# Scores of a query block as three products and then three copies, heads 0 to 3 ranked in twos, and five gathers issued inside the query phase

## The chip, the cores and the metric

The kernel runs on one core of one Trainium2 chip. The metric is device time in microseconds (us) of one execution, and the time of a version is the median of several runs. The engines are named as in the profile: PE is TensorE (matrix products), DVE is VectorE, ACT is ScalarE, POOL is GpSimd, SP is SyncE, which only issues transfers. Each engine runs its own instructions in the order in which the program lists them; semaphores make one engine wait for another.

## The reference

One layer of a hybrid decoder for 336 tokens, all in fp32. A mixer (a Conformer convolution and a Mamba-2 SSD side by side) is followed by PEER, a mixer of experts that are looked up with product keys. The change touches PEER alone:

```python
def peer_block(xb, w_q, keys, U, V):
    T = xb.shape[0]
    q = (xb @ w_q).reshape(T, PEER_HEADS, 2, D_KEY // 2)
    s = jnp.einsum('thcd,hckd->thck', q, keys).astype(jnp.float32)
    s1, i1 = lax.top_k(s[:, :, 0], PEER_TOPK)
    s2, i2 = lax.top_k(s[:, :, 1], PEER_TOPK)
    cand = (s1[..., :, None] + s2[..., None, :]).reshape(T, PEER_HEADS, PEER_TOPK * PEER_TOPK)
    sc, f = lax.top_k(cand, PEER_TOPK)
    ids = (jnp.take_along_axis(i1, f // PEER_TOPK, axis=-1) * N_KEYS
           + jnp.take_along_axis(i2, f % PEER_TOPK, axis=-1))
    g = jax.nn.softmax(sc, axis=-1)
    act = jax.nn.gelu(jnp.einsum('thkd,td->thk', U[ids], xb).astype(jnp.float32), approximate=False)
    w = (g * act).astype(xb.dtype)
    return jnp.einsum('thk,thkd->td', w, V[ids])
```

There are 8 heads with two halves each, 128 keys in each half, 16,384 experts, and 16 experts for each head and token, so 128 picks for each token. A row of U and a row of V have 1024 numbers.

## The kernel before

The mixer takes the first 527 us and isn't touched. PEER needs 320 of the tokens, and the kernel serves them in two ways. 128 *gathered* tokens (and 8 more, packed sixteen picks to a column) get their experts' rows by indirect transfers: for one pick of each of the 128 tokens a gather (L1159) brings 128 rows of U and V side by side, 1 MB, into one of five buffers `wuv`; VectorE makes the dot with the token (`pick_dot`, L1317), ScalarE takes the Gelu of it (L1319) and multiplies it by the softmax weight (L1322), and VectorE adds the weighted V rows to `ygat` (`pick_sum`, L1327). That is 137 steps. The other 184 *dense* tokens go through all experts: TensorE multiplies 128 blocks of U (512 KB each, L1429), ScalarE takes the Gelu into `S` (L1431), a mask with the weights is multiplied in, and TensorE multiplies 128 blocks of V (L1531).

**Query phase** (the loop over `j` of 16 blocks, 8 heads by 2 halves). A block of `w_q` (512 KB, from the SP queue) is split into a high half `wh`, made by ScalarE (L249), and a low half `wl`, made by POOL in four pieces of 128x256 (L253). TensorE makes 16 products of 128x320 with `wh` and 8 with `wl` (L182) into a PSUM tile `pj`; ScalarE copies that to `qT` (L1202). Then TensorE multiplies it by the keys, once for each of three tiles of tokens: the gathered 128, 128 dense ones, and 64 more (tile `psc`, L1206). ScalarE copies each of the three to SBUF (L1208): to `sco` for the gathered tokens, to `sall` for the others. All three products share one PSUM tile, and the program writes product, copy, product, copy; a product that writes `psc` waits for the copy of the product before it.

**Ranking.** `top16` (five steps of VectorE, L1061 to L1069) ranks the gathered tokens' scores as each block comes. After block 7, `heads_tasks(0)` works on heads 0 to 3: the sums of the two halves (`cand`), their top 16, the ids and the softmax weights (`gid` at L1136, `ggw`). Then `ahead(0)` issues the first gathers on POOL. The gathered tokens' heads 4 to 7 and the dense tokens' rankings (`topk_tasks(1)`, `topk_tasks(2)`) follow in the U phase.

**U phase.** Between the U blocks a `Feed` hands out VectorE's tasks (rankings and pick steps) by their cost, so many for each block: `NU = (42, 26, 35)` says how many picks fall to the first 84 U blocks, the other 44, and the first part of the V phase; the remaining 34 come last. A gather's buffer is free when the sum of the pick five before it has run. U outputs go to six PSUM banks in turn. U blocks land in eight tiles `pre` and a ring of eight `eraw` slots; from block 25 on every odd block is issued on ScalarE's queue (L1412). A dependency written by hand keeps every ranking of dense tokens behind the first cast to `gid` (`early[0]`), and one keeps each pick's Gelu behind the last score copy (`scored`).

A scheduler with a simulated timeline sets the order of instructions on each engine out of this program; it is the order below.

## Time and profile before

| | |
|---|---|
| median of 3 runs | 1280.56 us (1278.71, 1280.62, 1280.56) |
| the profiled execution | 1278.62 us, its span 1276.8 us |
| granted TensorE clock, mean | 0.995 of full speed |
| query phase | from about 529 us; U phase to 929 us, V phase behind it |
| TensorE busy | 1257.3 us of the span |
| VectorE, ScalarE, GpSimd busy | 961.7, 520.4, 595.6 us |

The profile is of one execution. Its rows give start and duration in us, the engine, the line of the kernel, the operation, what it writes and reads, and how many instructions a row holds; in brackets is how long the engine stood idle before and what ended that. A matmul of fp32 has two records for one product; TensorE is pipelined, so the distance of two starts, not the duration, is what a product costs.

### The profile page before, as it was taken

Reading aid. Unit: us, or ns where it says so; the run is one execution under the profiler, and the core shown is the slowest. Engines: PE = TensorE matmul, PEld = TensorE weight load, DVE = VectorE, ACT = ScalarE, POOL = GpSimd, SP = SyncE. Lnnn points to the kernel's source line nnn. Section 1 sums busy time; section 2 is a strip of 40 time slices with the busy share of each in tenths; the row PEclk is TensorE's granted clock in tenths of the full one; section 3 lists DMA queues with packets and bytes.
Section 4 is the critical chain, followed back from the end, with each engine's and each line's share of the span. In section 5 each row is a group of like instructions: output and inputs, shape, how many; then the busy total and the mean of one; then the engine's idle time right before and its main releaser. Section 6 shows DMA issues by size and latency. Waiting matters only on the chain.

```text
span 1276.8 us, 23637 instructions
## 1 busy us (share of the span) xinstructions
PE 1257.3 (98%) x8953; PEld 1214.0 (95%) x8953; DVE 961.7 (75%) x2121; ACT 520.4 (41%) x1308; POOL 595.6 (47%) x595
## 2 busy tenths in 40 slices
PE   9999999999999999999999999999999999999997
PEld 7989999999889999999999999999999999999997
DVE  6888889888977335549999978888888888545555
ACT  6778777887766444544232222222210111001102
POOL 2487777887795766975132232223322322122110
PEclk9899999999999999999999999999999999999999
DMA  6435454344434444765989999999999999999994
GB/s 248 166 130 194 158 190 169 140 175 170 145 126 149 149 150 149 255 243 210 372 321 422 421 420 420 420 420 420 420 421 420 420 421 419 397 421 420 419 421 158
DMA packets 85618, 373.82 MB, mean 293 GB/s; under 512 B 9585, under 2 KB 15089, under 8 KB 65921
## 3 DMA queue, kind: packets, MB, share of 16 engines
q1 hardware_dynamic: 48048, 166.87, 34.9%
q0 software_dynamic: 19584, 142.62, 26.9%
q10 hardware_dynamic: 17872, 62.84, 12.2%
q8 instruction: 70, 1.15, 0.4%
q14 instruction: 44, 0.35, 0.1%
HBM read 359.24 MB, written 13.05 MB: 292 GB/s over the span
## 4 chain that ended last, share of the span: by engine, by line
PE 81%; DVE 15%; DMA 2%; ACT 1%; issue 1%; POOL 1%; ACTq 0%; DVEq 0%
PE pj L182 32%; PE va L1531 25%; PE pj L1429 15%; DVE wuv L1317 2%; DVE ygat L1327 2%; PE pg L1457 2%; DVE pcv L525 1%; PE pst L182 1%; DMA wuv<-in_peer_uv_dram,gid 1%; PE po L182 1%; PE py L182 1%; PE pq L182 1%; DMA wdt<-in_w_dt_dram 1%; DVE st L718 1%; DVE si L1066 1%
## 5 line engine op out<-in xcount | busy, mean ns | idle before, releaser
L1159 POOL DMA_INDIRECT wuv<-in_peer_uv_dram,gid x136 | 166.2, 1222 | 478.3 <-PE va L1531 133.7
L253 POOL TENSOR_TENSOR wl<-wraw,wh 128x256 fp32r<-128x256 f32 (+1 forms) x202 | 289.9, 1455 | 109.5 <-ACT wh L249 64.9
L1531 PE MATMUL va<-S,eraw 128*128 128x184 f32 x2048 | 325.4, 320 | 0.0
L1531 PEld LDWEIGHTS va<-S,eraw 128*128 128x128 f32 x2048 | 318.9, 190 | 0.9 <-issue 0.9
L1429 PE MATMUL pj<-nd,eraw 128*128 128x184 f32 x1792 | 290.1, 321 | 1.8 <-DMA eraw<-in_uT_dram 1.7
L1429 PEld LDWEIGHTS pj<-nd,eraw 128*128 128x128 f32 x1792 | 278.8, 190 | 2.6 <-ACT S L1431 2.2
L182 PE MATMUL pj<-ah,wh 128*128 128x336 f32 (+1 forms) x768 | 242.6, 327 | 1.5 <-ACT xg L225 1.2
L182 PE MATMUL pj<-al,wh 128*128 128x336 f32 (+1 forms) x768 | 232.6, 316 | 0.0
L1327 DVE SCALAR_TENSOR_TENSOR ygat<-wuv,scg,ygat 128x1024 f32<-128x1024 f32 x128 | 164.0, 1281 | 73.5 <-ACT scg L1322 72.9
L1317 DVE SCALAR_TENSOR_TENSOR wuv<-wuv,x2m 128x1024 f32<-128x1024 f32 x128 | 156.2, 1221 | 56.6 <-DMA wuv<-in_peer_uv_dram,gid 54.2
L1319 ACT ACTIVATE scg<-scg 128x1 f32<-128x1 f32 x136 | 27.3, 202 | 416.6 <-DVE wuv L1317 297.8
L249 ACT CAST wh<-wraw 128x1024 fp32r<-128x1024 f32 x125 | 131.0, 1049 | 78.3 <-PE pj L182 55.7
L182 PEld LDWEIGHTS pj<-ah,wh 128*128 128x128 f32 x768 | 145.4, 190 | 7.1 <-issue 2.7
L182 PEld LDWEIGHTS pj<-al,wh 128*128 128x128 f32 x768 | 145.1, 190 | 0.7
L182 PE MATMUL pj<-ah,wl 128*128 128x336 f32 (+1 forms) x768 | 138.5, 315 | 1.9 <-POOL wl L253 1.9
L525 DVE SCALAR_TENSOR_TENSOR pcv<-ch,vec,pcv 128x320 f32<-128x320 f32 x232 | 127.6, 550 | 10.8 <-ACT pcv L523 8.1
L182 PEld LDWEIGHTS pj<-ah,wl 128*128 128x128 f32 x768 | 120.3, 189 | 3.0 <-POOL wl L253 2.9
L1431 ACT ACTIVATE S<-pj 128x184 f32<-128x184 f32 x128 | 38.6, 316 | 109.7 <-PE pj L1429 100.1
L536 DVE SCALAR_TENSOR_TENSOR pj<-mcat,vec,pj 128x360 f32<-128x360 f32 x96 | 56.5, 590 | 5.5 <-ACT pj L534 5.1
L1468 DVE SCALAR_TENSOR_TENSOR S<-pg,S 128x232 f32<-128x232 f32 (+1 forms) x92 | 34.5, 417 | 14.3 <-PE pg L1457 10.4
L1322 ACT ACTIVATE scg<-scg,ggw 128x1 f32<-128x1 f32 x136 | 39.7, 294 | 6.2 <-PE va L1531 1.8
L1429 PE MATMUL pj<-nd,pre 128*128 128x184 f32 x256 | 42.0, 319 | 0.0
(392 smaller groups left out, 1693.9 us busy)
## 6 DMA issues: line engine op xcount, KB each, us to landing
wraw<-in_w_in_dram SPq DMA_DIRECT2D x80, 512.0 KB
eraw<-in_vE_dram SPq DMA_DIRECT2D x64, 512.0 KB
eraw<-in_vE_dram ACTq DMA_DIRECT2D x64, 512.0 KB
eraw<-in_uT_dram SPq DMA_DIRECT2D x60, 512.0 KB
eraw<-in_uT_dram ACTq DMA_DIRECT2D x52, 512.0 KB
st<-in_state_dram SPq DMA_DIRECT2D x8, 1024.0 KB
out_ssm_s_dram<-st SPq DMA_DIRECT2D x8, 1024.0 KB
wraw<-in_w_mo_dram SPq DMA_DIRECT2D x16, 512.0 KB
```

What stands on the lines that cost most here:

```text
L182: i_ = nc.tensor.matmul(*a_, **kw)
L249: (nc.vector.tensor_copy if on_dve else nc.scalar.copy)(h, src)
L253: (nc.gpsimd if on_pool else nc.vector).tensor_tensor(l[:, q:q + m], src[:, q:q + m], h[:, q:q + m].bitcast(F32), op=OP.subtract)
L525: nc.vector.scalar_tensor_tensor(to, in_, sc, eights(acc), op0=OP.mult, op1=OP.add)
L536: nc.vector.scalar_tensor_tensor(o, cat[:, w:w + n], wv, o, op0=OP.mult, op1=OP.add)
L1159: i_ = nc.gpsimd.indirect_dma_start(out=u, out_offset=None, in_=ia["peer_uv"], in_offset=bass.IndirectOffsetOnAxis(ap=gid[:, c:c + 1], axi ...
L1317: nc.vector.scalar_tensor_tensor(u[:, :D], u[:, :D], 1.0, x2m if c < NPICK else x2e, op0=OP.mult, op1=OP.mult, accum_out=w)
L1322: nc.scalar.activation(w, w, AF.Copy, scale=ggw[:, c:c + 1])
L1327: nc.vector.scalar_tensor_tensor(a_, u[:, D:], scg[:, c:c + 1], a_, op0=OP.mult, op1=OP.add)
L1429: i_ = nc.tensor.matmul(p[:, :ND], raw[:, k, :], nd[:, k, :], start=(k == 0), stop=(k == KD - 1))
L1431: nc.scalar.activation(Sv(b), p[:, :ND], AF.Gelu)
L1531: i_ = nc.tensor.matmul(va[k // 2][:, k % 2], raw[:, k, :], Sv(b), start=(b == 0 and k % 2 == 0), stop=(b == 127), skip_group_check=True)
```

## The change

The three score products of a block are made one after the other, into a tile of its own in the two banks of tag `y`, and the three copies follow. `heads_tasks` takes a number of heads: heads 0 and 1 are worked on after block 3, heads 2 and 3 after block 7, heads 4 to 7 where they were. Gathers 0 to 2 are issued after block 3 and gathers 3 and 4 after block 7. The first six pick steps stand ahead of the `Feed`. The dense tokens' rankings are kept behind the second cast to `gid`. `NU` gives 47 picks to the first 84 U blocks, 26 to the others and 34 to the first part of the V phase, so 30 come last.

```diff
+HB0 = 2
+SOON = {3: (0, 1, 2), 7: (3, 4)}
+NSOON = 6
...
-NU = (42, 26, 35)
+NU = (47, 26, 34)
...
-                tc.add_manual_dep(i_.ins, early[0], mybir.DependencyInfo(mybir.DependencyClass.NoSync,
+                tc.add_manual_dep(i_.ins, early[1], mybir.DependencyInfo(mybir.DependencyClass.NoSync,
...
-        def heads_tasks(h0):
+        def heads_tasks(h0, HG):
...
-            p = misc([128, 3, NK], "psc")
+            p = ps.tile([128, 3, NK], F32, name="psc", tag="y", bufs=2)
+            ups = [64 * (j // (2 * n)) for n in heads_of]
             for i, (t0, L) in enumerate(KTILES):
-                n, up = 2 * heads_of[i], 64 * (j // (2 * heads_of[i]))
-                nc.tensor.matmul(p[:, i], qT[:, t0 - up:t0 - up + 128], keys[:, j, :], start=True, stop=True)
+                nc.tensor.matmul(p[:, i], qT[:, t0 - ups[i]:t0 - ups[i] + 128], keys[:, j, :], start=True, stop=True)
+            for i, (t0, L) in enumerate(KTILES):
+                n, up = 2 * heads_of[i], ups[i]
                 s_ = sall[i][:, j % n] if i else kp.tile([128, NK], F32, name="sco", bufs=9)
                 scored = nc.scalar.copy(s_[up:up + L], p[up:up + L, i]).ins.name
...
-            if j == 2 * HG - 1:
-                for _, f_ in heads_tasks(0):
+            if j in (HG - 1, 2 * HG - 1):
+                for _, f_ in heads_tasks(j // 2 - HB0 + 1, HB0):
                     f_()
-            if j == 2 * HG - 1:
-                ahead(0)
+            if j in SOON:
+                for n in SOON[j]:
+                    pend[n] = gather(COLS[n])
...
+        for _, f_ in take(NSOON):
+            f_()
         t1, t2 = topk_tasks(1), topk_tasks(2)
-        bg = mixin(t1[:-1] + t2[:-5] + t1[-1:] + t2[-5:-1], take(NU[0] - 4 - LATER)) + take(4) + t2[-1:]
-        bg += mixin(heads_tasks(HG), take(LATER))
+        bg = mixin(t1[:-1] + t2[:-5] + t1[-1:] + t2[-5:-1], take(NU[0] - 4 - LATER - NSOON)) + take(4) + t2[-1:]
+        bg += mixin(heads_tasks(HG, PH - HG), take(LATER))
```

The lines of the changed kernel are three higher from the top of the file on, and five to eight higher behind the score products: L1159 is L1162 there, L1206 is L1209, L1208 is L1213, L1319 is L1325, L1322 is L1328, L1429 is L1437 and L1431 is L1439.

What this does to the order, at three places. First POOL in the query phase, before: `wl` are the pieces of the low halves (four a block), `x2m` and `x2e` are the tokens of the picks, and the last row are all gathers. The row of 28 pieces begins with block 5.

```order
L253 TENSOR_TENSOR wl<-wraw,wh 128x256 x28
L1054 TENSOR_TENSOR x2e<-x2e,wuv 128x512
L253 TENSOR_TENSOR wl<-wraw,wh 128x256 x4
L1054 TENSOR_TENSOR x2e<-x2e,wuv 128x512
L253 TENSOR_TENSOR wl<-wraw,wh 128x256 x12
L1159 DMA wuv<-in_peer_uv_dram,gid 128x2048 x136
```

And the same stretch of POOL in the changed kernel:

```order
L256 TENSOR_TENSOR wl<-wraw,wh 128x256 x8
L1057 TENSOR_TENSOR x2e<-x2e,wuv 128x512
L256 TENSOR_TENSOR wl<-wraw,wh 128x256 x2
L1057 TENSOR_TENSOR x2e<-x2e,wuv 128x512
L256 TENSOR_TENSOR wl<-wraw,wh 128x256 x6
L1162 DMA wuv<-in_peer_uv_dram,gid 128x2048 x5
L256 TENSOR_TENSOR wl<-wraw,wh 128x256 x28
L1162 DMA wuv<-in_peer_uv_dram,gid 128x2048 x131
```

Five gathers have moved from behind all low halves to the place between block 8 and block 9; the first of them waits for the ids of heads 0 and 1, the other four for nothing more, and the 28 pieces of blocks 9 to 15 stand behind them.

Second, PE at block 9's low products in the changed kernel (`ah,wl` are products with a low half, `ah,wh` and `al,wh` those with a high half; the products of L1437 are those of U block 5):

```order
L185 MATMUL pj<-al,wh 128x320
L1437 MATMUL pj<-nd,pre 128x184 x2
L185 MATMUL pj<-ah,wl 128x320 x2
L1437 MATMUL pj<-nd,pre 128x184 x2
L185 MATMUL pj<-ah,wl 128x320 x2
L1437 MATMUL pj<-nd,pre 128x184 x2
L185 MATMUL pj<-ah,wl 128x320 x2
L1437 MATMUL pj<-nd,pre 128x184
L185 MATMUL pj<-ah,wl 128x320 x2
```

U block 5 is laid between the low products of block 9. Before, U blocks 1, 3 and 5 stood at earlier places of the query phase; in the changed kernel U block 5 is the only one ahead of the query phase's last blocks.

Third, ACT behind the last scores in the changed kernel (`S` are the evacuations of U blocks, `scg` from `scg` the Gelu of a pick, `scg` from `scg,ggw` its weight):

```order
L1439 ACTIVATE S_7393<-pj 128x184 x2
L1213 COPY sco<-psc 128x128
L1213 COPY sall_6447<-psc 128x128
L1213 COPY sall_6448<-psc 64x128
L1325 ACTIVATE scg<-scg 128x1 x5
L1328 ACTIVATE scg<-scg,ggw 128x1 x5
L1439 ACTIVATE S_7393<-pj 128x184 x5
L1325 ACTIVATE scg<-scg 128x1
L1328 ACTIVATE scg<-scg,ggw 128x1
L1439 ACTIVATE S_7393<-pj 128x184 x2
```

The Gelus of picks 0 to 4 stand in one row behind the last score copy; then come five evacuations, and the Gelu of pick 5, which waits for VectorE's dot, with the further evacuations behind it. On VectorE six rankings of gathered tokens (blocks 0 to 5) stand ahead of the first cast to `gid` now; before, the rankings of about twelve blocks did.

## The prediction

> **What bounds the kernel now.** First the page's busy shares, then the waits of TensorE, then the stretches from 527 us on, the only ones the change touches. The rows of a stretch give its length, then busy time (and instructions) of PE, PEld, DVE, ACT and POOL, the granted clock, the DMA share and GB/s.
>
> ```profile
> PE 1257.3 (98%) x8953; PEld 1214.0 (95%) x8953; DVE 961.7 (75%) x2121; ACT 520.4 (41%) x1308; POOL 595.6 (47%) x595
> ...
> PE pj L182 <- POOL wl L253: 2.3, 5, 0.7
> PE pj L1429 <- DMA eraw<-in_uT_dram: 1.7, 2, 1.2
> ...
> 527.00:596.00 69.00, 68.74 (x482) 67.88 (x482) 42.99 (x196) 34.06 (x83) 50.53 (x64) 1.00 0.63 225
> 596.00:620.00 24.00, 24.00 (x164) 24.00 (x163) 23.93 (x137) 9.26 (x31) 4.89 (x5) 1.00 0.98 393
> ...
> 680.00:700.00 20.00, 18.79 (x121) 18.54 (x120) 19.90 (x63) 6.52 (x20) 4.16 (x5) 1.00 1.02 421
> ...
> 720.00:740.00 20.00, 19.44 (x132) 18.65 (x131) 17.27 (x32) 5.73 (x21) 4.29 (x4) 1.00 1.02 423
> 740.00:1200.00 460.00, 460.00 (x3506) 454.58 (x3506) 342.32 (x573) 69.25 (x266) 122.73 (x97) 1.00 1.02 418
> ```
>
> TensorE is the bound: 98% of the span, and in the 460 us from 740 it has no idle time at all, although DMA is full there too (1.02, 418 GB/s). The change removes no product from it. So it can gain only what TensorE waits for between 527 and 740, and lose only by a new wait of TensorE. VectorE has 26 us free in the query phase (69.00 less 42.99) and next to none from 596 to 620 (23.93 of 24.00).
>
> **Scores in threes.** A score product is two records of a matmul.
>
> ```profile
> 577.86 2.29 PE L1206 MATMUL psc<-keys,qT 128*128 128x128 f32 x12
> 579.98 0.41 PE L182 MATMUL pj<-ah,wh 128*128 128x320 f32 x1
> ...
> 583.02 0.38 PE L1206 MATMUL psc<-keys,qT 128*128 128x128 f32 x2
> 583.16 0.39 PE L182 MATMUL pj<-ah,wl 128*128 128x320 f32 x1
> 583.39 0.38 PE L1206 MATMUL psc<-keys,qT 128*128 128x128 f32 x2
> ...
> 588.01 0.76 PE L1206 MATMUL psc<-keys,qT 128*128 128x128 f32 x4
> 588.73 0.42 PE L182 MATMUL pj<-ah,wh 128*128 128x320 f32 x1
> ...
> 529.03 0.31 PE L182 MATMUL pj<-ah,wh 128*128 128x320 f32 x1
> 531.38 0.74 PE L182 MATMUL pj<-ah,wl 128*128 128x320 f32 x4
> ```
>
> From 529.03 to 531.38 lie sixteen projection products: 2.35 / 16 = 0.147 us each. A single score between two of them, 583.02 to 583.39, takes 0.37 - 0.147 = 0.223. So most of the 48 scores cost no wait: ScalarE copies one while TensorE does projections. A wait shows only where nothing else lay between: six scores from 577.86 to 579.98 took 2.12 against 6 x 0.223 = 1.34 (0.78 lost), two from 588.01 to 588.73 took 0.72 against 0.45 (0.27 lost). With a product of its own slot for each tile and the copies behind, both go: **-1.0 us**. The other 40 scores gain nothing, since the counts of products and copies stay; ScalarE's copies come in another order only, on an engine that is busy 34.06 of 69.00.
>
> **Ranking in twos, and five gathers ahead.** The rows of VectorE and GpSimd (POOL), before:
>
> ```profile
> 533.34 2.13 DVE L1039 COPY wuv<-xT 128x1024 f32<-128x1024 f32 x1
> 546.02 0.29 DVE L1061 MAX8 sv<-sco 128x8 f32<-128x128 f32 x1 [4.63 <-ACT sco L1208]
> 548.44 0.29 DVE L1069 FIND_INDEX8 si<-sv,sco 128x8 uint32<-128x128 f32 x1
> 579.18 0.94 DVE L1083 TENSOR_TENSOR cand<-sv 128x480 f32<-128x480 f32 x1
> 598.25 0.19 DVE L1136 CAST gid<-idh 128x64 int32<-128x64 f32 x1
> 608.41 1.21 DVE L1317 SCALAR_TENSOR_TENSOR wuv<-wuv,x2m 128x1024 f32<-128x1024 f32 x1
> 626.22 1.27 DVE L1327 SCALAR_TENSOR_TENSOR ygat<-wuv,scg,ygat 128x1024 f32<-128x1024 f32 x1
> ...
> 544.18 5.59 POOL L253 TENSOR_TENSOR wl<-wraw,wh 128x256 fp32r<-128x256 f32 x8
> 572.57 1.29 POOL L1054 TENSOR_TENSOR x2e<-x2e,wuv 128x512 f32<-128x512 f32 x1
> 574.17 2.81 POOL L253 TENSOR_TENSOR wl<-wraw,wh 128x256 fp32r<-128x256 f32 x4 [0.31 <-ACT wh L249]
> 578.19 3.23 POOL L253 TENSOR_TENSOR wl<-wraw,wh 128x256 fp32r<-128x256 f32 x4
> 598.73 1.14 POOL L1159 DMA_INDIRECT wuv<-in_peer_uv_dram,gid  x1 [7.54 <-DVE sv L1061]
> 603.90 0.94 POOL L1159 DMA_INDIRECT wuv<-in_peer_uv_dram,gid  x1 [0.30 <-issue]
> 628.25 0.94 POOL L1159 DMA_INDIRECT wuv<-in_peer_uv_dram,gid  x1 [23.41 <-DVE sv L1068]
> ```
>
> Now the ids of four heads are ready at 598.4, five gathers go out until 604.8, the first sum is at 626.2, and only then the sixth gather. Afterwards, by the order shown above, POOL issues the five gathers between the low halves of block 8 and of block 9; they wait for the ids of heads 0 and 1, and 28 pieces (blocks 9 to 15) queue behind them. TensorE needs those pieces. That is the change's **new wait**, and I price it by two clocks.
>
> TensorE reaches the low products of block 9 (those laid between the products of U block 5) after 200 projection products and 27 scores from the 529.03 row, in the new order, with some 1.6 us of small products: 529.0 + 200 x 0.147 + 27 x 0.223 + 1.6 = 566.1.
>
> POOL ends the low halves of blocks 5 and 6 at 544.18 + 5.59 = 549.8; two pieces of x2e and blocks 7 and 8 follow, 2 x 1.29 + 2 x 2.81 = 8.2, so it is free at 558.0. The ids: VectorE is free for ranking at 535.5 (533.34 + 2.13). In the new order six pairs of rankings and the ranking of heads 0 and 1 stand ahead of the ids. A pair takes 2.7 us (546.02 to 548.73): 16.2, of which the last 1 us stands behind. Four heads took 19.1 us (579.18 to 598.25) with some 6 us of other ranking inside, so 13.1; two take between half of it, 6.5, and all of it. I take 8, near the half, since most of the instructions are one for each head. 535.5 + 16.2 - 1 + 8 + 0.8 for score copies that are waited for = **559.5**. Five gathers took 6.1 us (598.73 to 604.84): POOL is free at 565.6, and the first of block 9's pieces is ready 0.7 later, at 566.3. Against 566.1 that is a wait of 0.2, and then a piece takes 0.70 to 0.81 where TensorE needs, with U block 5's products between them, 0.60 to 0.9: some 0.2 for each of the first four, and block 10 is covered again, since a block takes TensorE 24 x 0.147 + 3 x 0.223 = 4.2 and POOL 2.8. Together **+1.2 us**; the ends are 0 (ids at 558.0, TensorE covered by a piece) and +6.3 (ids at 564.6, if two heads cost what four do).
>
> A rule of the Trainium skill speaks against this place: "GPSIMD Engine Reference", section 1, has GpSimd share its SBUF interfaces with VectorE, with contention where VectorE reads two SBUF inputs. The trace agrees: four pieces took 3.23 beside the two-input 128x480 of 579.18 and 2.81 without. Five dots, which read two inputs, now fall beside the 28 pieces; by the rule block 9 is some 0.4 later, and the new wait would be +1.6 in place of +1.2.
>
> **What the earlier start gives.** From 590 on everything that uses gathered rows starts earlier: the first sum stands right behind the last score copy (about 604, against 626.2), five dots are done in VectorE's free time, and 5.2 MB of rows (12.5 us at 418 GB/s) move out of a stretch that is full into one at 225 GB/s. But the only waits of TensorE that it can take away are two:
>
> ```profile
> 690.78 10.21 PE L1429 MATMUL pj<-nd,eraw 128*128 128x184 f32 x64 [1.21 <-DMA eraw<-in_uT_dram]
> ...
> 701.16 25.10 PE L1429 MATMUL pj<-nd,eraw 128*128 128x184 f32 x160
> 726.74 8.04 PE L1429 MATMUL pj<-nd,eraw 128*128 128x184 f32 x48 [0.48 <-DMA eraw<-in_uT_dram]
> ...
> 688.98 0.20 ACT L1319 ACTIVATE scg<-scg 128x1 f32<-128x1 f32 x1 [3.10 <-DVE wuv L1317]
> ```
>
> Both are U blocks that land late; half of them are issued on ScalarE's queue, which just before stood 3.10 us behind a Gelu that waited for a dot on VectorE. A lead of VectorE shortens such waits. Against it: 47 picks instead of 42 are laid into the first 84 U blocks, so the full stretch keeps about its rate of gathers. The gain lies between 0 and 1.7; the rows lean to neither, and I take one of two gone, **-0.9**.
>
> The gathers also meet the loads of w_q and of the first U blocks on the DMA engines, which are 63% busy in this phase. ScalarE's casts hide that, as they run up to two blocks ahead of TensorE; without that cover it would cost what a late load costs in the nearest row, up to 1.2 (the wait at 690.78), and I take nothing.
>
> Sum: -1.0 + 1.2 - 0.9 = **-0.7 us** on the profiled execution of 1278.62, so 1277.9. The four times of the kernel before (1278.62, 1278.71, 1280.56, 1280.62) have a mean of 1279.6, 1.0 above the profiled one; so I predict **1278.9**. The rest of the kernel keeps its length: TensorE has 460.00 of 460.00 from 740 to 1200, and one pick moved from the V phase to the U phase meets VectorE at 342 of 460.
>
> **Rivals.** (a) *All waits go and none comes.* If the ids are ready by 558.0, POOL is free at 564.1, ahead of TensorE's 566.1: -1.0 - 1.7 = -2.7, 1276.9. For it: VectorE's 26 us of free time, and U block 5 as cover. Against it: my id time is later, and the DMA is as full as before. Chance 0.20.
> (b) *Slower: the low halves come too late.* Each us that the ids come after 559.4 stops TensorE for a us at block 9; nothing is left to fill in, as U blocks 1 and 3, which stood between the blocks before, are gone from there. With ids at 564, five later than mine (two heads at the price of four), +5.8 - 1.0 - 0.9: 1283.5. For it: VectorE must first rank blocks 4 and 5, whose scores TensorE gives only by 553. Its chance 0.17; it decides the sign from ids at about 560.2 on.
> (c) *Slower: a Gelu holds the U phase's evacuations.* In the new order the Gelu of pick 5 stands on ScalarE behind seven evacuations; it waits for pick 5's dot, and TensorE fills its six banks in the meantime. From block 9 on it has 136 projection products, 21 scores and thirteen U blocks of 2.51 (25.10 for 160 records of 16 a block) before it lacks a bank: 566.1 + 20.0 + 4.7 + 32.6 = 623.4. I put the dot at about 613 (VectorE's 63 us of work from 535 to the fifth dot of before, some 6 more, and 8 of waits, an estimate). From 10 us later on it costs a us each; at 14 later, 1282.9. Chance 0.05.
> (d) *The change hides nothing.* The U waits at 690 and 726 stay: -1.0 + 1.2 = +0.2, 1279.8. For it: 1.02 of DMA before and after. Chance 0.19.
>
> **How the numbers follow.** My forecast has 0.33, the rivals 0.20, 0.17, 0.05 and 0.19, and 0.06 are left for a gain or loss not seen here. 0.2%, 2.6 us, is about what a measurement of this kernel can tell from no change. Faster by more: (a) and half the rest, 0.23; slower by more: (b), (c) and the other half, 0.25; the forecast and (d) lie within, 0.52. The range leaves out the far part of (b) and of (a): 1276.0 to 1283.5.
>
> **What would show it.** Right: the three scores of a block 0.67 apart from begin to end with no idle time on a copy; ids of heads 0 and 1 at 558 to 561; TensorE idle about 1 us on POOL between 565 and 572; one of the U waits gone. Wrong: ids after 562 or TensorE waiting over 3 us for low halves (b); a gap near 623 that ends with ScalarE's evacuation (c); new waits on U blocks in 600 to 660, where the sixth gather and those behind it now start, would make all of it wrong.

## The result, and the profile after

| | before | changed |
|---|---|---|
| median, same chip | 1280.28 us (1278.71 to 1280.62, 4 runs) | 1295.61 us (1293.24 to 1299.82, 4 runs) |
| ratio, 95% interval | | 1.0126 [1.0098, 1.0153] |
| profiled execution | 1278.62 us | 1295.67 us, its span 1293.9 us |

The change makes the kernel 1.3% slower, some 15 us, where 0.7 us less were forecast. Two executions of variants below, one of e6_nu42 (5046.5 us) and e18_again (3280.81 us), ran with TensorE slowed from end to end and are left out of every figure.

First the page's busy shares, the waits of TensorE from 527 us on (who waited for whom: us in total, times, the longest), and the stretches, with the columns of before:

```profile
PE 1261.3 (97%) x8953; PEld 1215.6 (94%) x8953; DVE 979.5 (76%) x2147; ACT 517.5 (40%) x1309; POOL 604.6 (47%) x595
...
PE psc L1209 <- ACT qT L1205: 6.9, 1, 6.9
PE pj L1437 <- DMA eraw<-in_uT_dram: 4.5, 2, 3.7
PE pg L1465 <- DVE oh L1461: 1.1, 2, 0.6
PE pj L1437 <- ACT S L1439: 0.9, 2, 0.6
PE pj L185 <- POOL wl L256: 0.8, 2, 0.4
PE pg L1465 <- DVE S L1476: 0.4, 1, 0.4
...
527.00:596.00 69.00, 61.27 (x417) 59.54 (x416) 64.62 (x224) 33.71 (x88) 56.78 (x64) 0.95 0.69 261
...
660.00:700.00 40.00, 36.25 (x233) 36.00 (x233) 38.79 (x89) 10.78 (x37) 13.66 (x10) 1.00 0.93 355
...
740.00:1200.00 460.00, 458.16 (x3504) 452.97 (x3503) 334.26 (x566) 67.07 (x267) 119.76 (x94) 1.00 1.01 414
```

TensorE's waits grew from 1.7 to 14.6 us, and the largest is one that the prediction does not contain: a score product waits 6.9 us for a copy of `qT` on ScalarE. A second reading gives the loss by place, as the start of the same TensorE product against before, both counted from the first product of the query phase: U block 13 of 128, behind the whole query phase in both kernels, comes 10.2 us late, block 38 15.6, and everything from the end of the U phase on 17.1 to 17.2. So in this execution some 10 us are lost in the query phase, 7 in the U phase (TensorE stands idle for 3.75 us between 660 and 700), none behind it. The rows around the big wait, VectorE and POOL first, then ScalarE, TensorE and the granted clock:

```profile
543.74 11.38 DVE L1086 TENSOR_TENSOR cand<-sv 128x240 f32<-128x240 f32 x1
568.10 0.16 DVE L1139 CAST gid<-idh 128x32 int32<-128x32 f32 x1
...
541.65 2.40 POOL L1027 TENSOR_TENSOR x2m<-x2m,wuv 128x1024 f32<-128x1024 f32 x1
544.01 5.60 POOL L256 TENSOR_TENSOR wl<-wraw,wh 128x256 fp32r<-128x256 f32 x8
...
553.44 1.42 POOL L256 TENSOR_TENSOR wl<-wraw,wh 128x256 fp32r<-128x256 f32 x2
561.33 2.96 POOL L256 TENSOR_TENSOR wl<-wraw,wh 128x256 fp32r<-128x256 f32 x4 [6.47 <-ACT wh L252]
568.55 1.15 POOL L1162 DMA_INDIRECT wuv<-in_peer_uv_dram,gid  x1 [4.26 <-DVE sv L1071]
...
573.73 0.94 POOL L1162 DMA_INDIRECT wuv<-in_peer_uv_dram,gid  x1 [0.30 <-issue]
574.70 25.42 POOL L256 TENSOR_TENSOR wl<-wraw,wh 128x256 fp32r<-128x256 f32 x28
...
559.67 0.32 ACT L228 ACTIVATE gh<-gh,rsT 128x32 f32<-128x32 f32 x1 [9.92 <-DVE gh L1141]
559.90 0.41 ACT L1205 COPY qT<-pj 128x320 f32<-128x320 f32 x1
560.21 1.04 ACT L252 CAST wh<-wraw 128x1024 fp32r<-128x1024 f32 x1
...
560.36 1.65 PE L1209 MATMUL psc<-keys,qT 128*128 128x128 f32 x6 [6.87 <-ACT qT L1205]
...
562.00:564.00 2.00, 2.00 (x10) 2.00 (x9) 2.00 (x12) 1.07 (x4) 2.00 (x4) 0.50 0.00 0
566.00:568.00 2.00, 2.00 (x15) 2.00 (x15) 1.98 (x15) 0.59 (x3) 0.00 (x0) 1.00 0.42 170
```

Read it from the top. VectorE's add of the candidates of heads 0 and 1 takes 11.38 us (heads 2 and 3: 0.4). It starts 0.3 us before POOL's `x2m` ends and ends at 555.12, just after POOL runs dry: fourteen POOL instructions, from 544.01 to 554.86, go by in between. So VectorE is late with `gh`; the softmax Exp of these heads stands on ScalarE ahead of a `qT` copy and waits 9.92 us for it; behind it stand the `qT` copy, for which TensorE waits 6.87 us, and the cast of the next `wh`, for which POOL waits 6.47. Then the granted clock is 0.50 for some 4 us more. The ids come at 568.1, and the gathers end at 574.7, ahead of block 9's low halves.

The early start did not reach the picks either. The first weighted sum, and the sixth gather that waits for it, in the changed kernel, and the first sum of e1_group, the kernel before with grouped scores alone:

```profile
621.88 1.26 DVE L1333 SCALAR_TENSOR_TENSOR ygat<-wuv,scg,ygat 128x1024 f32<-128x1024 f32 x1
623.41 0.95 POOL L1162 DMA_INDIRECT wuv<-in_peer_uv_dram,gid  x1 [23.29 <-DVE sv L1071]
```

```profile
605.88 1.26 DVE L1329 SCALAR_TENSOR_TENSOR ygat<-wuv,scg,ygat 128x1024 f32<-128x1024 f32 x1
```

Five gathers start 30 us earlier than before (568.6 against 598.7), but the first sum comes only 4 us earlier (621.9 against 626.2). The weights of picks 0 to 4 are ready at 610.8 (ScalarE's row of 609.81, 1.02 us long); VectorE then still works off rankings, most of them of dense tokens, which stand ahead of the sum in its order, without a pause until 621.9. In e1_group, where nothing is ranked or gathered early, the sum comes 16 us earlier than here.

### The profile page after: what moved, and what is told of

The parts are those of the page before. It is cut to its first block, busy times and chain, and to the rows that moved or that the text cites. A ratio compares the mean times of both kernels' runs of the same rounds, so it can differ in the third digit from the quotient of the medians.

```text
span 1293.9 us, 23666 instructions
## 1 busy us (share of the span) xinstructions
PE 1261.3 (97%) x8953; PEld 1215.6 (94%) x8953; DVE 979.5 (76%) x2147; ACT 517.5 (40%) x1309; POOL 604.6 (47%) x595
## 4 chain that ended last, share of the span: by engine, by line
PE 35%; DVE 11%; DMA 7%; POOL 1%; issue 1%; ACT 0%; DVEq 0%; ACTq 0%; POOLq 0%
PE va L1539 25%; PE pj L1437 9%; DMA wuv<-in_peer_uv_dram,gid 6%; DVE ygat L1333 3%; DVE wuv L1323 2%; PE pg L1465 2%; POOL wl L256 1%; DVE cand L1116 1%; DVE cand L1113 0%; DVE si L1069 0%; DVE si L1072 0%; DVE cand L1110 0%; DVE sv L1064 0%; DVE ci L1072 0%; DVE ci L1069 0%
## 5 line engine op out<-in xcount | busy, mean ns | idle before, releaser
L1162 POOL DMA_INDIRECT wuv<-in_peer_uv_dram,gid x136 | 169.8, 1249 | 490.2 <-PE va L1539 169.8
L256 POOL TENSOR_TENSOR wl<-wraw,wh 128x256 fp32r<-128x256 f32 (+1 forms) x202 | 295.6, 1483 | 102.7 <-ACT wh L252 71.3
L1437 PE MATMUL pj<-nd,eraw 128*128 128x184 f32 x1792 | 289.8, 321 | 4.6 <-DMA eraw<-in_uT_dram 4.5
L1437 PEld LDWEIGHTS pj<-nd,eraw 128*128 128x128 f32 x1792 | 278.8, 190 | 5.6 <-ACT scg L1325 5.0
L1325 ACT ACTIVATE scg<-scg 128x1 f32<-128x1 f32 x136 | 27.1, 202 | 454.2 <-DVE wuv L1323 286.2
L1439 ACT ACTIVATE S<-pj 128x184 f32<-128x184 f32 x128 | 37.5, 315 | 83.8 <-PE pj L1437 83.6
L1437 PE MATMUL pj<-nd,pre 128*128 128x184 f32 x256 | 41.7, 320 | 0.9 <-ACT S L1439 0.9
L1437 PEld LDWEIGHTS pj<-nd,pre 128*128 128x128 f32 x256 | 40.0, 190 | 1.4 <-ACT S L1439 1.4
```

Source lines behind the costliest of these rows:

```text
L256: (nc.gpsimd if on_pool else nc.vector).tensor_tensor(l[:, q:q + m], src[:, q:q + m], h[:, q:q + m].bitcast(F32), op=OP.subtract)
L1162: i_ = nc.gpsimd.indirect_dma_start(out=u, out_offset=None, in_=ia["peer_uv"], in_offset=bass.IndirectOffsetOnAxis(ap=gid[:, c:c + 1], axi ...
L1437: i_ = nc.tensor.matmul(p[:, :ND], raw[:, k, :], nd[:, k, :], start=(k == 0), stop=(k == KD - 1))
L1439: nc.scalar.activation(Sv(b), p[:, :ND], AF.Gelu)
```

## The experiments

Ratios are to the kernel before, run beside each variant on the same chip. "Lag" is how much later than before the same TensorE product starts in the profiled execution, counted as above from the first product of the query phase.

### Which part costs what

**e1_group**: the kernel before with the three products and then three copies alone.

> The kernel before with the three score products of a block in a tile of their own and the copies behind, and nothing else of the change. Both theories: the loss is in the early ranking, not here. 1278.5 to 1280.5, that is -1 to 0 against before; TensorE's longest wait between 527 and 600 under 0.5 us; the sums of four heads' candidates (128x480) take about 0.9 us.

1275.85 us, ratio 0.9976 [0.9966, 0.9985]. Lag -0.7 us at U block 13, behind the query phase, and -2.1 from mid U phase on. Its only wait on a load there:

```profile
PE pj L1431 <- DMA eraw<-in_uT_dram: 0.7, 1, 0.7
```

The wait near 690 us has gone. This part is a gain of some 3 us, more than was expected; the rest of the change loses about 18. More moved than the scores: the scheduler laid the U blocks behind the query phase (TensorE's first U product at 588.8 us, 536.5 before), the last score product starts at 597.4 instead of 618.9, and the first ids come at 583.2 instead of 598.3. So e1_group measures the grouping together with the order that follows from it.

**e5_nu47**: e1_group with the other split of the picks alone.

```diff
-NU = (42, 26, 35)
+NU = (47, 26, 34)
```

> The kernel with the score products in threes alone, and NU = (47, 26, 34) in place of (42, 26, 35): five picks more between the first 84 U blocks, nothing moved ahead of them. In the changed kernel TensorE lost 5 to 7 us again between 640 and 860 (waits for a U block near 690, for VectorE's masks near 790 to 832). Theory N (the picks laid in the U phase are too many for VectorE and the DMA): that loss comes back here, 1279.5 to 1283. Rival L (it follows from the late start of the U phase and from the early picks): 1275 to 1277, as without the edit.

1285.87 us, 1.0056 [1.0039, 1.0073]: ten more than e1_group, on theory N's side and above its range. The lag is -0.7 until 30% of the U phase, +5.4 at 60%, +6.6 at its end. A stretch, two rows of ScalarE's timeline, and VectorE's largest wait from 620 to 835 us:

```profile
740.00:780.00 40.00, 35.29 (x241) 34.42 (x240) 30.11 (x52) 8.11 (x33) 10.52 (x8) 0.91 1.02 420
...
750.96 0.20 ACT L1321 ACTIVATE scg<-scg 128x1 f32<-128x1 f32 x1 [5.31 <-DVE wuv L1319]
751.20 0.34 ACTq L1414 DMA_DIRECT2D eraw<-in_uT_dram  x1
...
DVE wuv L1319 <- DMA wuv<-in_peer_uv_dram,gid: 19.4, 14, 1.9
```

DMA is full (1.02), TensorE loses 4.7 of 40 us, and ScalarE stands 5.31 us in front of a pick's Gelu, with the issue of a U block behind it. Is it DMA, or VectorE's own work for each pick (a dot of 1.22 us and a sum of 1.28)? The last line says 19.4 us on gathers, where e1_group has none in this window. VectorE is busy for 179.7 of these 215 us, so it isn't full; it waits for transfers.

**e6_nu42**: the changed kernel with the old split, `NU = (42, 26, 35)`.

> The changed kernel with NU = (42, 26, 35) as before; ranking in twos and the five early gathers stay. Theory N: the waits behind 640 shrink, 1287 to 1291; the loss of some 10 us up to 600 stays. Rival L: 1293 to 1297.

1289.8 us (1288.6 to 1292.2, three runs), 1.0087 [1.0066, 1.0108]: in theory N's range. TensorE's waits:

```profile
PE pj L185 <- POOL wl L256: 4.2, 1, 4.2
PE pj L1437 <- ACT S L1439: 2.8, 3, 1.3
PE pj L1437 <- DMA eraw<-in_uT_dram: 2.7, 1, 2.7
PE pj L1437 <- ACT scg L1325: 1.7, 1, 1.7
```

Here the add took 0.58 us, ScalarE's Exp came early (550.4), the ids came at 563.05, and the cost is the forecast's own wait, on block 9's low halves, at 4.2 instead of 1.2.

**e7_behind** and **e8_behind42**: the changed kernel with all five gathers behind block 15's low halves, with 47 and with 42 picks. (The Exps of heads 0 to 3 are also written later in the program; the scheduler left them at their early place.)

```diff
-SOON = {3: (0, 1, 2), 7: (3, 4)}
+SOON = {15: (0, 1, 2, 3, 4)}
...
+            if not steps:
+                tc.add_manual_dep(i_.ins, lows[-1], mybir.DependencyInfo(mybir.DependencyClass.NoSync,
...
```

> The changed kernel with both things that wait for the early ranking taken out of the query phase's way: the Exp and weights of heads 0 to 3 are written behind block 15, and the five gathers stand on POOL behind the low halves of block 15. The ranking in twos stays where it is on VectorE. Theory: the query phase loses nothing against the kernel with the scores in threes (TensorE's waits in 530 to 600 under 1 us together); what is left is the U phase's loss of 5 to 7 us: 1279 to 1283. Rival (VectorE's own work in the query phase, slowed by POOL, holds TensorE in some other way): 1286 to 1295.

> As the one before it, with NU = (42, 26, 35). Theory N with both queues free: no loss left but for the six picks ahead, 1275 to 1278. Rival L (early picks or ranking cost the U phase): 1280 to 1284.

e7_behind: 1288.63 us (1285.6 to 1292.0), 1.0082 [1.0062, 1.0102], in the rival's range, but not by its mechanism: the lag at U block 13 is +0.6, and the loss comes later. e8_behind42: 1281.35 us, 1.0020 [1.0005, 1.0034], in rival L's range, in two groups: 1278.5 to 1281.4 (six) and 1284.3 to 1285.9 (four). No wait for low halves is left in either. The profile of e8_behind42 is of the upper group and has the add at 11.40 us:

```profile
PE psc L1221 <- ACT qT L1217: 6.9, 1, 6.9
PE pj L1451 <- DMA eraw<-in_uT_dram: 1.7, 1, 1.7
```

By ratios the whole splits in four: scores in threes -0.24%; early ranking and the six steps ahead of the `Feed`, with gathers out of the way (e1_group to e8_behind42) +0.44%; gathers ahead of block 9 (to e6_nu42) +0.67%; 47 picks (to the changed kernel) +0.39%, or in us about -3, +6, +9 and +5. Steps of one chain add up to the measured +1.26% by themselves, so that the sum proves nothing; for the first three steps the intervals of the two kernels lie apart, for the last (e6_nu42 and the changed kernel) they overlap. And the steps aren't pure: the profile of the changed kernel has the long add, that of e6_nu42 hasn't.

### Why VectorE is late

**e2_gap**: the changed kernel with a memset of 64x64 on POOL (0.15 to 0.18 us) ahead of the low halves of blocks 5 to 8.

```diff
+            if 5 <= j <= 8:
+                nc.gpsimd.memset(acce[64:, :64], 0.0)
```

> The changed kernel with four small memsets on POOL (64x64, they read no SBUF) laid between the low halves of blocks 5 to 8. Theory P (port): the candidate sum of heads 0 and 1, two inputs in SBUF, took 11.38 us because POOL went from one two-input instruction to the next without a gap, and DVE got its turn only when POOL ran dry. Then it ends at the first memset, behind block 5's pieces (546.8 to 548), takes about 3 to 4 us, and TensorE's 6.87 us wait for qT shrinks to under 1: 1283 to 1287. Theory O (the sum's own delay, an instruction fetch or a wait that the profile doesn't name): it stays at 11 us and ends near 555 whatever POOL does: 1294 to 1297.

1290.68 us, 1.0089 [1.0073, 1.0106], between the two theories. The add took 0.95 us, the Exp came at 552.56, no wait on `qT` was left. But the ids came at 564.13 all the same, and TensorE waited 3.8 us for low halves and 3.3 behind a Gelu (`scg`). This doesn't test the gap: the memsets lay at 543.75 and 549.38, and the add began at 545.70 and ended at 546.65, between them, when POOL's instruction in flight was done. What the run does show, as far as its one profile stands for its four executions, is the price of the change without the long add: still 0.89% of the 1.26.

**e3_psum**: the changed kernel, with one input of the add of heads 0 and 1 in PSUM.

```diff
+                s1 = misc([128, H_, 16], "s1p")
+                nc.vector.tensor_copy(s1, s2[:, :, 0])
...
```

> The changed kernel; the candidate sum of heads 0 and 1 takes its first input from PSUM (a DVE copy of 128x32 puts it there). Theory P: an instruction with one SBUF input isn't held, 0.4 us in place of 11.38; the Exp of heads 0 and 1 runs before 553, the ids are ready before 563, and TensorE waits under 2 us in 545 to 565, unless the next two-input instruction (the subtraction before the Exp) is held in its place, which then takes the 5 to 10 us. 1281 to 1288. Theory O: the copy or the sum still takes 11 us: 1294 to 1297.

1293.96 us, 1.0118 [1.0101, 1.0135], above theory P's range. The add took 0.40 us, and a cast behind it, an operation with one input, was held in its place until POOL ran dry; TensorE waited 3.2 us on `qT`:

```profile
545.26 6.67 DVE L1097 CAST sf<-si 128x256 bf16<-128x256 uint32 x1
```

**e4_late**: the changed kernel, with the softmax weights of heads 0 and 1, and so the Exp, behind block 15.

```diff
+                if h0 == 0:
+                    held.append(weights)
...
```

> The changed kernel with the subtraction, Exp and weights of heads 0 and 1 written behind block 15 in place of block 3; sum, ranking and gathers stay. Theory P: the sum is still held, 11 us or more, but nothing on ScalarE waits for it, so the 6.87 us wait for qT goes; POOL then doesn't run dry at 555, the sum is held until POOL's pieces of block 8 end (about 558), the ids come at about 571, the five gathers end at 577, and TensorE waits about 9 to 11 us for block 9's low halves instead: 1293 to 1299, no gain. Rival: with ScalarE free the loss is gone, 1281 to 1287, since the pieces of block 9 come in time.

1293.59 us, 1.0106 [1.0078, 1.0135]. The time is in the theory's range by luck: the add was not held (0.58), the ids came at 564.39 and not at 571, and TensorE waited 3.9 us for block 9's low halves and not 9 to 11. No wait on `qT` was left, but the interval overlaps the changed kernel's, so that taking the Exp away alone gained nothing that can be told from noise. The Exp is one carrier of VectorE's lateness, and POOL's queue, with the gathers in it, is another.

**e12_port** and **e15_probe**: the hold by itself, at the end of e1_group, 200 plain two-input adds, and 260 with the candidate add's operands, on VectorE beside back-to-back two-input subtractions on GpSimd. The loops of e12_port:

```diff
+            for n in range(n_pool):
...
+                tc.keep_in_program_order(nc.gpsimd.tensor_tensor(l_[:, q:q + 2], a3[:, q:q + 2],
...
+            for n in range(n_dve):
...
+                tc.keep_in_program_order(nc.vector.max(y_[:, 1000:1008], x_[:, :w_]))
+                tc.keep_in_program_order(nc.vector.tensor_tensor(y_[:, :240], x_[:, :240], x_[:, 240:480], op=OP.add))
```

> A measurement at the end of the kernel before with grouped scores: 300 two-input subtractions (128x256) back to back on GpSimd, and beside them 200 times on VectorE a MAX8 over 64 to 463 elements and a two-input add of 128x240. The output is the reference's, the extra work writes scratch tiles. Theory (a two-input operation of VectorE waits for the GpSimd instruction in flight, and now and then is held through many): most adds take 0.4 to 1.5 us, some 1 to 4 in 100 several GpSimd instructions (4 us or more). Rival 1 (a hold happens only at one phase of the two streams or for one operand form, not this one): none over 2 us. Rival 2 (GpSimd keeps the port as long as its instructions follow without a gap, always): nearly every add is held for tens of us.

> A measurement at the end of the kernel before with grouped scores: 450 two-input subtractions back to back on GpSimd (every ninth 128x1024, the others 128x256), and beside them 260 times on VectorE one to five MAX8 and the candidate add of two heads (128x240, both inputs repeated by a stride of zero). Extra work writes scratch tiles. With a plain add none of 200 was held over 0.79 us. Theory A (the form of the operands makes the hold possible, and chance decides): some of the 260 adds take 4 us or more. Theory B (it takes more than form and neighbour): none over 3 us.

The instructions of the add's line, with shortest, median and longest in ns, first of e12_port, then of e15_probe:

```profile
L1591 DVE TENSOR_TENSOR wl<-wraw x200: 381/585/785, 1273.4 to 1441.9; 128x240 f32<-128x240 f32 x100
```

```profile
L1593 DVE TENSOR_TENSOR wl<-wraw x260: 387/670/2571, 1273.6 to 1733.5; 128x240 f32<-128x240 f32 x130
L1586 POOL TENSOR_TENSOR wl<-wraw,wh x450: 716/769/2608, 1273.8 to 1705.3; 128x256 fp32r<-128x256 f32 x100, 128x1024 fp32r<-128x1024 f32 x50
```

All 200 adds of e12_port and 239 of the 260 of e15_probe ran beside GpSimd, and none of these 439 was held over more than about one GpSimd instruction (the longest, 2.57 us, began with a piece of 2.34). So e12_port's rival 1 and e15_probe's theory B have it, and the theories that make the hold easy to provoke fall; what it takes besides the neighbour stays open.

**e16_again, e17_again, e18_again**: e8_behind42 unchanged.

> e8_behind42 unchanged, profiled again. Theory (the hold is chance within one program): in some of the three new profiles the candidate add near 542.7 us takes under 1 us, TensorE does not wait 6.9 us on qT there, and that execution takes 1278 to 1282 us; where it is held, 1284 to 1286 us. Rival (the hold is fixed by the program, and the two groups of times are something else): all three held, with times in either group.

> The second of three more profiles of e8_behind42: the same as for e16_again, an add under 1 us goes with 1278 to 1282 us, and one of some 11 us with 1284 to 1286 us.

> The third of three more profiles of e8_behind42: the same as for e16_again, an add under 1 us goes with 1278 to 1282 us, and one of some 11 us with 1284 to 1286 us.

VectorE's candidate adds and TensorE's waits, of e16_again (1285.56 us) and of e17_again (1282.12 us):

```profile
544.09 11.39 DVE L1088 TENSOR_TENSOR cand<-sv 128x240 f32<-128x240 f32 x1
568.59 0.30 DVE L1141 CAST gid<-idh 128x32 int32<-128x32 f32 x1
...
PE psc L1221 <- ACT qT L1217: 6.9, 1, 6.9
```

```profile
543.10 0.59 DVE L1088 TENSOR_TENSOR cand<-sv 128x240 f32<-128x240 f32 x1
545.06 0.66 DVE L1086 TENSOR_TENSOR cand<-sv 128x32 f32<-128x32 f32 x1
545.91 0.60 DVE L1095 CAST sf<-si 128x256 bf16<-128x256 uint32 x1
564.29 0.16 DVE L1141 CAST gid<-idh 128x32 int32<-128x32 f32 x1
568.79 0.28 DVE L1095 CAST sf<-si 128x256 bf16<-128x256 uint32 x1
...
PE pj L1451 <- DMA eraw<-in_uT_dram: 3.0, 1, 3.0
PE psc L1221 <- ACT qT L1217: 1.6, 1, 1.6
```

Of the three, e16_again and e17_again count. One program, held once and once not: the program doesn't fix the hold, and in this sense it comes by chance. It costs 7.2 us at U block 13 (lag +7.8 against +0.6) and 2.5 at the end (+6.8 against +4.3), since the U phase's waits take part of it over. The 1282.12 lie 0.7 above e8_behind42's lower group, the 1285.56 within its upper one; that the two groups are the held and the unheld executions rests on three profiles. And e17_again shows what the early ranking costs without a hold: it ends at +4.3, e1_group at -2.1. Its waits are 1.6 us on `qT` and 3.0 on a load at 687 us, behind which the granted clock was 0.50 from 688 to 692 us.

### Can the early ranking be had for nothing?

**e9_freed**: e8_behind42, with the two Exps of heads 0 to 3 tied behind the last score copy.

```diff
+                if h0 < 4:
+                    tc.add_manual_dep(e_.ins, scored, mybir.DependencyInfo(mybir.DependencyClass.NoSync,
...
```

> The changed kernel with its five gathers behind block 15's low halves, 42 picks in the first stretch, and the softmax Exp of heads 0 to 3 held on ScalarE behind the last score copy. Theory (three carriers: the Exp ahead of qT copies, the gathers ahead of low halves, 47 picks): nothing of the change but the grouped scores is left in TensorE's way, so the query phase ends 0.5 to 1 us early, even if VectorE's add of the candidates is held again, and the median is 1275 to 1278 us. Rival 1 (ranking in twos is itself dearer, since VectorE's longer work holds qT or score evacuations): +2 us or more at the end of the query phase with the Exp out of the way, median 1279 to 1283. Rival 2 (early gathers cost later, by DMA time taken from the U weights): query phase early, but a U loss as without the Exp dep, 1279 to 1282.

1286.56 us (1280.5 to 1288.3), 1.0044 [1.0024, 1.0065]: above all three ranges, the theory's by 9. The profile is of 1287.68 us; two of the seven took 1280.5 and 1281.7, and why isn't known. The add was held longest here, 14.22 us, and the query phase did not feel it (lag +0.3 us at U block 6; e1_group has +0.9 there). Then the lateness surfaced at the first Gelu, and the lag was 8.1 at block 13 (ScalarE, then TensorE):

```profile
597.98 1.28 ACT L1343 ACT_TABLE_LOAD   x1
611.35 0.20 ACT L1343 ACTIVATE scg<-scg 128x1 f32<-128x1 f32 x1 [12.09 <-DVE wuv L1341]
...
615.19 3.13 PE L1455 MATMUL pj<-nd,pre 128*128 128x184 f32 x9 [6.21 <-ACT S L1457]
```

**e13_freed_picks**: e9_freed, with the first picks some seven U blocks later, their Gelus and the two Exps tied behind the evacuation written last, and 40, 27 and 36 picks.

```diff
+            tc.add_manual_dep(i_.ins, evac[-1] if n < 8 else scored,
...
+        feed = Feed([(14.0, lambda: None)] + [(0.5, f_) for f_ in held] + bg, SB - 1)
```

> As e9_freed (gathers behind block 15's low halves, no Exp ahead of score copies), and the first picks come some seven U blocks later, their Gelus and the two Exps on ScalarE behind the evacuation of the U block written last; 40, 27 and 36 picks in the three stretches. Theory (the ranking in twos costs nothing by itself; each loss was an in-order queue in which TensorE's next input stood behind a late VectorE result): the 6.2 us wait on S at 615 us goes, the query phase ends 0.5 to 1 us early, and the median is 1275 to 1279 us. Rival (a late ranking is paid in any place, for VectorE itself is the bound of that stretch): over 1282 us, with the wait at a later place of VectorE's chain.

1292.04 us (1285.7 to 1293.1), 1.0086 [1.0053, 1.0118]: the rival's side. The add was held again (14.17 us). Now the first pick's multiplication by its softmax weight held the evacuations; TensorE waited 6.7 us for them, and later 3.4 for loads:

```profile
630.96 0.29 ACT L1345 ACTIVATE scg<-scg,ggw 128x1 f32<-128x1 f32 x1 [20.68 <-DVE ggw L1161]
```

So the attempt moved the wait a third time and did not remove it. VectorE has next to no slack from 566 to 660 us (in e13_freed_picks 63.52 of 64 us busy to 630 and 29.53 of 30 behind it), and none in e1_group either (63.93 and 29.76). That no other order would do it isn't shown.

### How many picks the first stretch bears

**e10_nu44, e11_nu40, e14_nu4028**: e1_group with `NU` (44, 26, 35), (40, 26, 35) and (40, 28, 35).

> The kernel before with grouped scores, and 44 picks instead of 42 in the first stretch. With 42 it was 1275.85 us, with 47 1285.87. Theory (the DMA engines are full in the first U stretch: 84 blocks of 0.524 MB and n picks of 1.049 MB at 420 GB/s last 215 us with 44 and 222 us with 47, against 211 us of matmuls): about +4 us, 1278 to 1281 us. Rival (VectorE's or ScalarE's queue order at 47 is what costs, a step and not a slope): within 1 us of 42, or all of the 10.

> The kernel before with grouped scores, and 40 picks instead of 42 in the first stretch, two more among the last ones. Theory (DMA full): 84 blocks and 40 picks take 205 us at 420 GB/s, below the 211 us of the matmuls, and what is left of the U waits (0.74 us of DMA wait on eraw at 42) goes: 1275 to 1276 us, unless two more picks in the last stretch cost there. Rival (42 is no edge): within 0.3 us of 1275.85.

> The kernel before with grouped scores, 40, 28 and 35 picks in the three stretches. With 40, 26 and 35 the U phase ended 3.3 us early (2.2 with 42), but the two picks more at the end cost 4.2 us there. Theory (transfers bound both ends: two picks fewer in the first stretch take the last DMA wait away, and two more in the second must find room at full DMA): U phase 1 to 3 us early and no wait at the end, 1274.5 to 1277 us. Rival (the second stretch is full too): a wait of 2 us or more there or on the first V blocks, 1277 to 1281 us.

| picks in the first stretch | median us | ratio, 95% interval | lag at the U phase's end | lag at the end |
|---|---|---|---|---|
| 40 (two more last) | 1281.68 | 1.0025 [1.0014, 1.0036] | -3.3 | +2.9 |
| 40 (two more in the second) | 1275.87 | 0.9971 [0.9960, 0.9982] | -3.6 | -3.4 |
| 42 (e1_group) | 1275.85 | 0.9976 [0.9966, 0.9985] | -2.1 | -2.1 |
| 44 | 1280.96 | 1.0007 [0.9993, 1.0020] | +2.0 | +2.0 |
| 47 (e5_nu47) | 1285.87 | 1.0056 [1.0039, 1.0073] | +6.6 | +6.6 |

The median of 44 hides two groups, 1276.2 to 1278.5 (four) and 1280.8 to 1282.4 (six); its lags are of 1280.76, in the upper one. e10_nu44's and e14_nu4028's medians are within the ranges of their theories, e11_nu40's is the exception that its theory names.

The U phase's end moves the same way at every step, as transfers in a full stretch would have it; VectorE waits 20.7 us on gathers from 620 to 835 us at 44 and 19.4 at 47, and not at all at 42 (e1_group). But the wait that carries it differs: at 47 a load, at 44 a mask on VectorE, and at 40 with two more picks left for the end it is the finish behind the V phase. TensorE's largest waits of e10_nu44, e11_nu40 and e14_nu4028:

```profile
PE pg L1459 <- DVE oh L1455: 3.6, 1, 3.6
```

```profile
PE prd L1546 <- ACT sqd L1545: 4.0, 1, 4.0
```

```profile
PE prd L1546 <- ACT sqd L1545: 0.4, 2, 0.2
```

In e14_nu4028 the last line is TensorE's only wait from 527 us to the end. It and e1_group, which can't be told apart by their medians, are the versions that beat both kernels.

## Why the prediction was wrong

The forecast was 1278.9 in a range to 1283.5, and its dearest rival ended at 1283.5 too: each loss was priced alone, and three came together. Two of the prediction's own signs of being wrong came: ids after 562, and, where `qT` didn't hold TensorE first, over 3 us of waiting for low halves.

- **Scores in threes, -1.0.** About right: e1_group has -0.7 behind the query phase, with no wait between scores. But "the other 40 scores gain nothing" is wrong: with the order that follows from the grouping, the ids come 15 us earlier and the first sum 20 (605.9 against 626.2). One U wait went with it, so that this part alone gave more than the whole forecast. The prediction looked for that gain in the early gathers.
- **"ScalarE's copies come in another order only, on an engine that is busy 34.06 of 69.00."** This sentence is the first step that failed. Half busy is no answer for an engine that works in order: the Exp of heads 0 and 1 stood among these copies, bound to VectorE's `gh`, and nothing that stood behind it was named. In the changed kernel's profile it cost 6.9 us and some 2 more at half clock. Where VectorE isn't held it costs nothing or little (e6_nu42: no wait on `qT`; e17_again: 1.6). It is the longest wait and not the largest loss: e2_gap, without it, is still 0.89% slower than before, which leaves some 5 us of the 16 for it, an estimate from the two ratios.
- **Ids at 559.5, taken "near the half".** They came at 563.05 to 564.39 in e2_gap, e4_late and e6_nu42, where the add was not held, and at 568.1 in the changed kernel, where it was. The upper bound, 564.6, was the better value. Beside busy POOL the casts, the two-input operations and the small operations with one number (TENSOR_SCALAR) of the ranking can take longer, by up to the GpSimd instruction in flight (the cast 0.60 against 0.28, the short add 0.66 against 0.17 to 0.29; in e6_nu42 two TENSOR_SCALAR of 128x32 1.32 and 1.33 against 0.17); MAX8, FIND_INDEX8 and MATCH_REPLACE8 take 0.27 to 0.29 either way. The prediction counted such a wait for the 28 pieces of POOL only, none for VectorE.
- **New wait on low halves, +1.2, bounds 0 to 6.3.** The mechanism was right, the size wrong: 3.8, 3.9 and 4.2 us in e2_gap, e4_late and e6_nu42, within the bounds. That is rival (b), which had 5.8 for ids at 564 (4.5 later than 559.5, and not five). The sum has a slip as well: its parts, 0.2 and four times 0.2, make 1.0 and not 1.2. In the changed kernel's profile it shows as 0.8 only, since the wait on `qT` had put TensorE back already.
- **"47 picks instead of 42 ... so the full stretch keeps about its rate of gathers."** The other step that failed: alone it costs 10 us (e5_nu47 against e1_group). Five early gathers take five picks out of the stretch only if their transfers end earlier. In e5_nu47 nothing starts earlier, so its 10 is the whole price; in the changed kernel, where five start at 568, it was 5 to 6 by the medians (e6_nu42 to the changed kernel, intervals that overlap). The check was in the rows: 84 U blocks of 0.524 MB and 42 picks of 1.049 MB at 420 GB/s take 210 us, and 84 blocks take TensorE 84 x 2.51 = 211. There was room for none.
- **U waits, -0.9, from a first sum "right behind the last score copy (about 604, against 626.2)".** It came at 621.9, 12.6 us behind that copy (609.3), since VectorE's order had rankings ahead of it. So the lead of 22 us that the gain rests on was 4. In the changed kernel new waits came: 4.5 us on loads, 0.9 on evacuations, 1.5 on masks. Nothing shows that these follow from the late sum.
- **Rival (c), a Gelu ahead of evacuations,** did not decide the changed kernel (0.9 us on S), but e9_freed and e13_freed_picks show it at its full size once the earlier carriers are gone.
- **The Trainium skill's rule** on the shared interface ("GPSIMD Engine Reference", section 1), weighed at +0.4 by GpSimd's slowdown, named the right pair and I priced the wrong side: the cost lay in VectorE's waits. The skill's "SBUF — State Buffer", section "Summary: rules for kernel authors", has the second of the two to issue block until the first one finishes. The 439 adds of the probes agree, with one instruction's length at most; the held operations, of 6.67 to 14.22 us, do not, since they lasted over a row of instructions.

What stays open: what sets off the hold. It struck the add in five profiles (the changed kernel, e8_behind42, e9_freed, e13_freed_picks, e16_again), a cast in e3_psum, and no operation at that place in five others (e2_gap, e4_late, e6_nu42, e7_behind, e17_again). The add began 0.31 to 0.32 us before the end of the same POOL instruction in the changed kernel, e8_behind42 and e9_freed, where it was held, and as long before it in e4_late and e7_behind, where it was not; so that distance does not decide it. That a gap on POOL ends the hold is argued from the six held operations, which all ended 0.15 to 0.27 us behind POOL's last instruction before a gap; no run put a gap into one of them. And why the early ranking makes a load late without a hold (e17_again, 3.0 us) is not shown.

## What to carry to other kernels

When work is moved ahead, write down for each of its instructions what stands behind it on its engine, small ones on half-idle engines above all: one Exp of 0.32 us in front of a `qT` copy stopped TensorE for 6.9 us, five gathers in front of low halves for 3.8 to 4.2. A transfer that starts early gains only if what consumes it comes early too: look for the consumer's place in its own engine's order. When a stage's transfers and its products take the same time (here 210 and 211 us), transfers added to it are paid (here 2 to 2.5 us for each pick, by the medians), and a split of work over stages is a sum to be made before the change. A part that gains should be tried alone: grouping the scores was worth 3 us, and the rest of the change hid it under 18.

## What the hardware showed that wasn't expected

A cast, a two-input operation or a TENSOR_SCALAR of VectorE on SBUF beside a GpSimd stream normally waits for at most the instruction in flight (it took 0.4 to 1.3 us in the kernel, up to 2.6 beside a 128x1024). Now and then, in one and the same program, it is held until GpSimd runs dry: adds 11 to 14 us, over fourteen or more instructions, and a cast 6.67 us. And the wait of 6.9 us cost TensorE more than its length: its granted clock was 0.50 from 560 to 564 us, and 1.00 again from 566.
